# Halved additions for a pass's last operand, a unit issued in two parts, and two turns put with other work

## The chip, the core and the metric

The kernel runs on one core of a Trainium2 chip. A core has a matrix engine (PE, with its weight loads shown as PEld), a vector engine (DVE), a scalar engine (ACT), a general one (POOL) and a queue that issues the transfers (SP). Each has its own queue of instructions, runs it in order, and waits for the others through semaphores. The metric is the device time of one execution in microseconds (us), as a median of several runs. Beside the timed runs there is one profiled execution, whose span and time are given below.

## The reference

The kernel computes two layers of an encoder trunk for one sequence of 512 tokens of width 1024, all in float32. Cut to what matters here:

```python
for i in range(DEPTH):                        # 2 layers
    h = rms_norm(x, attn_norm[i])
    proj = h @ w_in[i]                        # one projection, its columns shared out
    mix = diff_attention(...) if i % 2 == 0 else gla_attention(...)
    cross = memory_cross_attention(mem_q, mem, mem_norm[i], w_mem_kv[i], mem_qk_norm[i])
    x = x + concatenate([mix, cross]) @ w_out[i]
    h = rms_norm(x, ffn_norm[i])
    x = x + conv_ffn(h, w_up[i], conv_w[i], conv_b[i], w_down[i])
# conv_ffn: u = h @ w_up, a causal convolution of width 3, silu(g) * a, and then @ w_down
# memory_cross_attention: 256 memory tokens, normalised, then @ w_kv gives keys and values
```

The inner width of the feed-forward part is 2816, that is 22 blocks of 128 columns for each of `a` and `g`.

## The kernel before

**Products.** Every large product is made of three: an operand is split into a rounded part (`hi`, written by ACT) and the remainder (`lo`, a subtraction on DVE), and PE adds hi x hi, hi x lo and lo x hi in PSUM. For weights, `split_weights` does this (L255 on ACT, L258 on DVE); for the combined weights below it is `combined` (sums on POOL at L287 to L290, roundings at L291 and L294, remainders at L292 and L295). A weight tile has 1024 columns, six of each kind are kept (`WB`), and a new block is made when PE has used an old one up (`make_block`, called from `freed` and `refill`).

**The feed-forward part** (`ffn`) runs in three passes over the inner width, of 4, 4 and 3 double blocks (`HALVES`). A pass first makes its inner operands: for each double block q, `up` multiplies (L387 to L389, in `product`), `conv` applies the convolution (L1166 to L1170), ACT the silu (L1329), and DVE multiplies (L1330). Then `down` multiplies by `w_down` and adds to x.

**The seven products.** Except in layer 0's last pass, and for one of the last pass's four output pairs in layer 1, a 2 x 2 block of `down` is computed with seven products instead of eight. That takes sums of the operand blocks: `combine` forms four sums of 256 columns into a tile `tsum` of 1024 (L1199 to L1202), and `parts_of` splits that tile (L1191 on ACT, L1192 on DVE). The sums are made on POOL, but on DVE for the last double block of a pass (`V if q == base + nq - 1 else ADD`). Of the seven steps, number 0 uses the second inner block's left half, 1 and 2 the first block's halves, and 3, 4, 5 and 6 use the sums q[3], q[0], q[1] and q[2]. Those four are called the mixed steps here.

**The order in `down`.** The output has four pairs of blocks (c = 0 to 3), and each has a unit of seven steps (21 products of 256 columns, L1247, routine `seven`) for every double block m. Pair c holds four PSUM banks; c and c + 2 use the same ones. The units are issued as follows: all of pair 0 but the last, pair 1's first, pair 0's last, the rest of pair 1, then pairs 2 and 3. When a pair's last unit has been issued, `decode` adds its four banks to x (L1256 on ACT, L1257 to L1264 on DVE), after which the banks are free. `release` follows each unit and lets `refill` make further weight blocks.

**Layer 0's attention.** PE's work is written out by hand in `SCRIPT`. A number pops that many microseconds' worth of projection units off a queue of work (`Filler`; a unit is six products of 512 columns, L365 to L367). Letters stand for attention work: `L` and `M` the logits of a group (L771), `T` its turn (four transposes on PE, L222, then a copy on ACT, L800), `V` its values (L812, which read that copy), `N` a normalisation (ACT squares at L422, sums and scales on DVE), `P` the transposes of the next head, `a` the memory operands. The queue holds, in this order, the values' projection, the second queries and keys, the memory's keys and values (`kv`, two blocks of four units), and further ones. At the end of that projection's first block a hook calls `token_rsqrt`, which computes the memory's scales (two transposes on PE, a sum at L468 on DVE, then ACT and DVE); the outputs of both blocks are scaled by them.

**What sets the order.** Only PE's queue is in the order of the program (`manual_schedule(engines={PE})`). For ACT, DVE, POOL and SP a planner orders the instructions ahead of time, by its own cost estimates and with program order as the priority. So an instruction that it takes to be waiting can be overtaken by later ones, and an order once planned is kept on the chip.

Of the kernel before, what the change touches and what calls it, by code (L numbers as in the profile page):

```python
# [21 lines left out]
S = 512  # L22
# [17 lines left out]
    17.75 P0 3.9  # L40
    L0 M1 a3 3.4 P1 5.05 a0 0.97
    1.94 a1 T0
    L2 M3 a2 3.57
    T1 4.86 N2 V0 T2 N3 V1 12.33
    L4 P2 4.55 P3 1.62 V2 T3 2.27 T4
    L5 M6 s0 V3 b1 2.6 V4 1.3 T5 1.3
    L7 M8 3.5 T6 F0 3.64 b0
# [135 lines left out]
def trunk(ctx, tc, head_d, x_t, mem_t, wpack, cols_a_d, cols_d, conv_d, gate_d, rel_bias, diff_lambda, consts, onehot, out):  # L183
    nc = tc.nc
    mm = nc.tensor.matmul
    V, A, G = nc.vector, nc.scalar, nc.gpsimd
# [23 lines left out]
    def blk(b, w=128):  # L210
        return slice(w * b, w * b + w)
# [140 lines left out]
    def gemm(sh, sl, nb, key, w, evac, hook=None, late=False, spare=False):  # L352
        got, open_ = [], {}

        piece = [q[0] for q in plan].index(key)

        def unit(b, k0, k1):
            if not got:
                got.extend(weights(key, True))
            if k0 == 0:  # L360
                open_[b] = bank("tp" if spare and b == 0 else "lg" if late and b > 1 else "mm")[:, :w]
            p = open_[b]
            for k in range(k0, k1):
                hi, lo = got[k]
                mm(p, sh[k][:, blk(b)], hi, start=k == 0, stop=False)  # L365
                mm(p, sh[k][:, blk(b)], lo, start=False, stop=False)  # L366
                mm(p, sl[k][:, blk(b)], hi, start=False, stop=k == KT - 1)  # L367
                if b == nb - 1:
                    freed(piece, k)
            if k1 == KT:  # L370
                if hook is not None and b == 0:
                    hook()
                evac(b, open_.pop(b))
        units = [(b, k) for b in range(nb) for k in range(0, KT, 2)]
        if late:
            units.sort(key=lambda u: u[0] == nb - 1 or u[1] == KT - 2)
        for b, k in units:
            F.add(6 * w / 2370.0, lambda b=b, k=k: unit(b, k, k + 2))
# [24 lines left out]
    r_mem = perm.tile([128, 2], F32, name="r_mem")  # L403
# [60 lines left out]
    def token_rsqrt(tag, sq, nb, y, on_dve=False):  # L464
        p, ss = bank(tag), small("ss")[:, :nb]
        for b in range(nb):
            transpose(p[:, blk(b)], sq[:, blk(b)])
        V.reduce_sum(ss, p[:, :128 * nb].rearrange("p (b n) -> p b n", b=nb), axis=AX.X)  # L468
        return rsqrt(ss, nb, 1.0 / D, on_dve, y=y)
# [9 lines left out]
    E = mybir.EngineType  # L479
# [106 lines left out]
    def mem_kv(l):  # L586
        hs, ls = [None] * KT, [None] * KT
        km = [None]

        def operands(ks=range(KT)):  # L590
            if l == 0 and km[0] is None:
                mem_squares()
            if km[0] is None:
                km[0] = xtile().rearrange("p (b n) -> p b n", b=2)
            for k in ks:
                if k % 2 == 0:
                    mh, ml = split_tiles()
                c = blk(k % 2, 256)
                hs[k], ls[k] = mh[:, c], ml[:, c]
                split(hs[k], ls[k], memT[k // 2][:, c], c_mem(l, k))  # L600

        def ev(b, p):
            A.activation(km[0][:, b], p[:, :256], AF.Copy, scale=r_mem[:, b:b + 1])
            A.activation(vm[l][:, b], p[:, 256:], AF.Copy, scale=r_mem[:, b:b + 1])

        def keys(tag="lg"):
            F.need(f"kv{l}")
            p = bank(tag)
            for hp in range(2):
                for b in range(2):  # L610
                    transpose(p[:, 256 * hp + 128 * b:256 * hp + 128 * b + 128], km[0][:, b, blk(hp)])
            A.activation(kmT[l].rearrange("p a b -> p (a b)"), p, AF.Copy, scale=c_mk(l))
        gemm(hs, ls, 2, ("kv", l), 512, ev,
             (lambda: token_rsqrt("lg", mem_acc[0], 2, r_mem)) if l == 0 else None)
        F.add(0.0, lambda: group_norm(None, km[0], 2, 4, 64))
        F.mark(f"kv{l}")
        return operands, keys
# [79 lines left out]
    def diff_layer(pool, mix, acc):  # L697
# [154 lines left out]
        for key in ORDER:  # L852
# [19 lines left out]
            "N": lambda i: norms(i // 2, i % 2), "a": lambda i: ops[0]((2 * i, 2 * i + 1)),  # L872
            "b": lambda i: ops[1]((2 * i, 2 * i + 1)), "k": lambda i: keys[i]("sm"),
            "q": lambda i: ma.queries() if i else (F.need("v2"), ma.norm()),
            "l": lambda i: ma.logits(i), "t": ma.turn, "v": lambda i: ma.values(i, "sm"),
            "s": lambda i: scales.pop(i)(), "X": lambda i: load_x(x_t),
            "O": lambda i: last.append(out_proj(0, mix, 1, acc, 5)), "!": lambda i: F.flush()}
        do(SCRIPT, doing)
# [270 lines left out]
    def ffn(pool, l, acc):  # L1149
# [40 lines left out]
        def parts_of(t, hi, lo):  # L1190
            A.copy(hi, t)  # L1191
            V.tensor_sub(lo, t, hi.bitcast(F32))  # L1192
# [3 lines left out]
        def combine(b2, b1, bh, bl, fh, fl, E):  # L1196
            t = pool.tile([128, 2 * S], F32, name="tsum", bufs=1)
            q = [blk(i, 256) for i in range(4)]
            E.tensor_sub(t[:, q[0]], b1[:, right], b1[:, left])  # L1199
            E.tensor_sub(t[:, q[1]], b2[:, right], t[:, q[0]])  # L1200
            E.tensor_sub(t[:, q[2]], b2[:, right], b1[:, right])
            E.tensor_sub(t[:, q[3]], b2[:, left], t[:, q[1]])  # L1202
            h, lo = (pool.tile([128, 2 * S], F32R, name="mid2", bufs=9) for _ in range(2))
            parts_of(t, h, lo)
            two = lambda hi, lw, c: (hi[:, c], lw[:, c])
            return [(fh, fl), two(bh, bl, left), two(bh, bl, right), two(h, lo, q[3]),
                    two(h, lo, q[0]), two(h, lo, q[1]), two(h, lo, q[2])]

        place = [(2, left), (0, left), (0, right), (1, left), (1, right), (2, right), (3, left)]
        steps, close = (1, 2, 0, 5, 6, 3, 4), {2: 0, 5: 2, 6: 3, 4: 1}  # L1210

        def down(base, nq, mids, pairs, tags, last, acc2):
            first = used[0]
# [21 lines left out]
            def release(c, m):  # L1235
                nonlocal live
                piece = first + c
                if m == nq - 1 or m % 2:
                    live -= 1 if whole[c] else 2
                    refill()  # L1240

            def seven(c, m):
                for i in steps:
                    b, h = place[i]
                    (hi, lo), (bh, bl) = made[first + c][m][i], mids[m][i]
                    for t, (w, v) in enumerate(((hi, bh), (hi, bl), (lo, bh))):
                        mm(banks[c][b][:, h], w, v, start=b not in seen[c], stop=m == nq - 1 and t == 2 and i in close)  # L1247
                        seen[c].add(b)
                release(c, m)
                if m == nq - 1:  # L1250
                    made[first + c] = None
                    decode(c)
# [35 lines left out]
                        made[first + c] = None  # L1288
                return
            refill()  # L1290
            seq = [(0, m) for m in range(nq - 1)] + [(1, 0), (0, nq - 1)] + [(1, m) for m in range(1, nq)]
            seq += [(2, m) for m in range(nq)] + ([] if whole[3] else [(3, m) for m in range(nq)])
            for c, m in seq:
                if c not in banks:
                    start(c)
                seven(c, m)
            if whole[3]:
                start(3)
                while done[0] < first_of[first + 4]:
# [140 lines left out]
```

## Time and profile before

| what | value |
|---|---|
| median of 3 runs | 1156.9 us (1156.76 to 1157.95) |
| profiled execution, its own time | 1156.94 us |
| its span in the profile | 1153.9 us |
| PE busy | 1145.4 us (99%) |
| DVE busy | 871.9 us (76%) |
| ACT busy | 590.7 us (51%) |
| POOL busy | 196.5 us (17%) |

A row of the timeline gives the start from the span's beginning, the duration (both in us), the engine, the line of the kernel, the operation, what it writes and reads with sizes, and how many like it are merged; in brackets stands how long the engine was idle before it and for whom it waited. Matrix products overlap each other: the next may start before the bar of the last one ends, so idle time on PE is best read from the distance of two starts. A list of waits gives the sum in us, the number and the longest. The five closings of passes that use the seven products lie, by L1247's rows, at 328.9 to 370.8, 458.0 to 498.8, 883.0 to 924.3, 1011.5 to 1052.4 and 1117.8 to 1142.2 us.

### The profile page before, as it was taken

Reading aid. Unit: us, or ns where it says so; the run is one execution under the profiler, and the core shown is the slowest. Engines: PE = TensorE matmul, PEld = TensorE weight load, DVE = VectorE, ACT = ScalarE, POOL = GpSimd, SP = SyncE. Lnnn points to the kernel's source line nnn. Section 1 sums busy time; section 2 is a strip of 40 time slices with the busy share of each in tenths; the row PEclk is TensorE's granted clock in tenths of the full one; section 3 lists DMA queues with packets and bytes.
Section 4 is the critical chain, followed back from the end, with each engine's and each line's share of the span. In section 5 each row is a group of like instructions: output and inputs, shape, how many; then the busy total and the mean of one; then the engine's idle time right before and its main releaser. Section 6 shows DMA issues by size and latency. Waiting matters only on the chain.

```text
span 1153.9 us, 16645 instructions
## 1 busy us (share of the span) xinstructions
PE 1145.4 (99%) x6311; PEld 986.5 (85%) x6311; DVE 871.9 (76%) x1450; ACT 590.7 (51%) x1027; POOL 196.5 (17%) x230
## 2 busy tenths in 40 slices
PE   9999999999999999999999999999999999999998
PEld 7888888888889888988888888988888988899887
DVE  8576778688689677977677637777887977797777
ACT  6676687555354344434457634435644444443442
POOL 0000000001543125500000000000144403370340
PEclk9999999999999999999999999999999999999999
DMA  8522242233214322243252220333241442233312
GB/s 294 169 80 86 79 142 74 59 106 115 87 59 143 110 76 80 101 135 103 69 179 71 97 98 9 108 122 113 77 124 38 130 143 73 68 93 132 93 45 101
DMA packets 39661, 117.81 MB, mean 102 GB/s; under 512 B 4767, under 2 KB 7256, under 8 KB 39582
## 3 DMA queue, kind: packets, MB, share of 16 engines
q1 hardware_dynamic: 39150, 116.37, 31.4%
q8 instruction: 49, 0.80, 0.3%
q10 hardware_dynamic: 432, 0.39, 0.1%
q14 instruction: 30, 0.25, 0.1%
HBM read 112.54 MB, written 4.21 MB: 101 GB/s over the span
## 4 chain that ended last, share of the span: by engine, by line
PE 77%; DVE 12%; POOL 5%; ACT 3%; DMA 2%; issue 2%; ACTq 0%; DVEq 0%; POOLq 0%
PE ps_mm L365 6%; PE ps_mm L367 6%; PE ps_mm L366 6%; PE ps_mm L387 5%; PE ps_mm L388 5%; PE ps_mm L389 5%; PE ps_lg L1247 4%; PE ps_sm L387 3%; PE ps_sm L388 3%; PE ps_sm L389 3%; PE ps_tp L1247 3%; PE ps_tp L222 3%; PE ps_mm L1247 2%; PE ps_lg L387 2%; PE ps_lg L389 2%; PE ps_lg L388 2%
## 5 line engine op out<-in xcount | busy, mean ns | idle before, releaser
L258 DVE TENSOR_TENSOR wlo<-raw,whi 128x1024 fp32r<-128x1024 f32 (+4 forms) x174 | 194.4, 1128 | 75.6 <-ACT whi L255 74.7
L255 ACT CAST whi<-raw 128x1024 fp32r<-128x1024 f32 (+4 forms) x174 | 168.1, 976 | 112.7 <-PE ps_sm L388 29.7
L365 PE MATMUL ps_mm<-whi,xsh 128*128 128x512 f32 (+2 forms) x328 | 126.4, 385 | 0.0
L367 PE MATMUL ps_mm<-whi,xsl 128*128 128x512 f32 (+2 forms) x328 | 123.0, 375 | 0.0
L366 PE MATMUL ps_mm<-wlo,xsh 128*128 128x512 f32 (+2 forms) x328 | 122.8, 374 | 0.0
L387 PE MATMUL ps_mm<-xsh,whi 128*128 128x512 f32 x278 | 109.3, 393 | 0.0
L388 PE MATMUL ps_mm<-xsl,whi 128*128 128x512 f32 x278 | 108.3, 390 | 0.0
L389 PE MATMUL ps_mm<-xsh,wlo 128*128 128x512 f32 x278 | 108.3, 389 | 0.0
L387 PE MATMUL ps_sm<-xsh,whi 128*128 128x512 f32 x218 | 84.8, 389 | 0.0
L388 PE MATMUL ps_sm<-xsl,whi 128*128 128x512 f32 x218 | 84.8, 389 | 0.0
L389 PE MATMUL ps_sm<-xsh,wlo 128*128 128x512 f32 x218 | 84.8, 389 | 0.0
L365 PEld LDWEIGHTS ps_mm<-whi,xsh 128*128 128x128 f32 x328 | 61.7, 188 | 11.4 <-issue 1.0
L367 PEld LDWEIGHTS ps_mm<-whi,xsl 128*128 128x128 f32 x328 | 61.7, 188 | 11.3
L366 PEld LDWEIGHTS ps_mm<-wlo,xsh 128*128 128x128 f32 x328 | 61.8, 188 | 10.1
L387 PE MATMUL ps_lg<-xsh,whi 128*128 128x512 f32 x160 | 62.2, 389 | 0.0
L388 PE MATMUL ps_lg<-xsl,whi 128*128 128x512 f32 x160 | 62.2, 389 | 0.0
L389 PE MATMUL ps_lg<-xsh,wlo 128*128 128x512 f32 x160 | 62.2, 389 | 0.0
L387 PE MATMUL ps_tp<-xsh,whi 128*128 128x512 f32 x160 | 62.2, 389 | 0.0
L388 PE MATMUL ps_tp<-xsl,whi 128*128 128x512 f32 x160 | 62.2, 389 | 0.0
L389 PE MATMUL ps_tp<-xsh,wlo 128*128 128x512 f32 x160 | 62.2, 389 | 0.0
L389 PEld LDWEIGHTS ps_mm<-xsh,wlo 128*128 128x128 f32 x278 | 52.2, 188 | 11.0
L388 PEld LDWEIGHTS ps_mm<-xsl,whi 128*128 128x128 f32 x278 | 52.2, 188 | 10.7 <-DVE xsl L346 0.4
(382 smaller groups left out, 2833.3 us busy)
## 6 DMA issues: line engine op xcount, KB each, us to landing
raw<-in_wpack_dram SPq DMA_DIRECT2D x178, 512.0 KB, 3.5
xt<-in_x_t_dram SPq DMA_DIRECT2D x15, 256.0 KB, 5.3
raw<-in_wpack_dram SPq DMA_DIRECT2D x15, 256.0 KB, 3.2
raw<-in_wpack_dram SPq DMA_DIRECT2D x8, 384.0 KB, 3.1
xres<-xt SPq DMA_DIRECT2D x8, 256.0 KB, 3.3
xt<-xres SPq DMA_DIRECT2D x8, 256.0 KB, 5.3
out_dram<-xt SPq DMA_DIRECT2D x7, 256.0 KB, 2.0
bt<-bias_d SPq DMA_DIRECT2D x6, 256.0 KB, 4.2
```

The lines of the kernel that those rows point to most:

```text
L222: nc.tensor.transpose(dst, src, ident[:n, :n])
L255: ins = A.copy(hi[:, c], raw[:, c])
L258: V.tensor_sub(lo[:, c], raw[:, c], hi[:, c].bitcast(F32))
L365: mm(p, sh[k][:, blk(b)], hi, start=k == 0, stop=False)
L366: mm(p, sh[k][:, blk(b)], lo, start=False, stop=False)
L367: mm(p, sl[k][:, blk(b)], hi, start=False, stop=k == KT - 1)
L387: mm(p, hi[:, blk(n)], bh, start=i == first, stop=False)
L388: mm(p, hi[:, blk(n)], bl, start=False, stop=False)
L389: mm(p, lo[:, blk(n)], bh, start=False, stop=i == last)
L1247: mm(banks[c][b][:, h], w, v, start=b not in seen[c], stop=m == nq - 1 and t == 2 and i in close)
```

## The change

There are three edits.

1. **Halves.** In `combine`, when the sums are made on DVE (the last double block of a pass), `parts_of` is called twice, on columns 0 to 511 (q[0], q[1]) and 512 to 1023 (q[2], q[3]), instead of once on all 1024. The steps' order becomes 1, 2, 0, 5, 4, 6, 3 (it was 1, 2, 0, 5, 6, 3, 4), so that the two mixed steps of the first half come before those of the second. This order holds in all units. A bank is now closed by step 3 where it was by step 4.
2. **A unit in two parts.** `seven` can issue some of its steps. Pair 0's last unit issues steps 1, 2 and 0; pair 1's second unit then issues its own 1, 2 and 0; then come the four mixed steps of pair 0's last unit and the four of pair 1's second. `release` and `decode` follow the second part.
3. **Turns.** In `SCRIPT` the turn T1 goes from its own place in the middle of a stretch of projection to behind V0, T2 and V1 go behind a further 2.6 us of projection, and a new letter `w` calls `token_rsqrt` for the memory's scales right behind V1; the hook in the memory's projection is dropped. The numbers between add up to 20.76 as they did.

```diff
@@ -40,8 +40,8 @@
     17.75 P0 3.9
     L0 M1 a3 3.4 P1 5.05 a0 0.97
     1.94 a1 T0
-    L2 M3 a2 3.57
-    T1 4.86 N2 V0 T2 N3 V1 12.33
+    L2 M3 a2 8.43
+    N2 V0 T1 N3 2.6 T2 V1 w 9.73
     L4 P2 4.55 P3 1.62 V2 T3 2.27 T4
     L5 M6 s0 V3 b1 2.6 V4 1.3 T5 1.3
     L7 M8 3.5 T6 F0 3.64 b0
@@ -610,8 +610,7 @@
                 for b in range(2):
                     transpose(p[:, 256 * hp + 128 * b:256 * hp + 128 * b + 128], km[0][:, b, blk(hp)])
             A.activation(kmT[l].rearrange("p a b -> p (a b)"), p, AF.Copy, scale=c_mk(l))
-        gemm(hs, ls, 2, ("kv", l), 512, ev,
-             (lambda: token_rsqrt("lg", mem_acc[0], 2, r_mem)) if l == 0 else None)
+        gemm(hs, ls, 2, ("kv", l), 512, ev)
         F.add(0.0, lambda: group_norm(None, km[0], 2, 4, 64))
         F.mark(f"kv{l}")
         return operands, keys
@@ -872,7 +871,7 @@
             "N": lambda i: norms(i // 2, i % 2), "a": lambda i: ops[0]((2 * i, 2 * i + 1)),
             "b": lambda i: ops[1]((2 * i, 2 * i + 1)), "k": lambda i: keys[i]("sm"),
             "q": lambda i: ma.queries() if i else (F.need("v2"), ma.norm()),
-            "l": lambda i: ma.logits(i), "t": ma.turn, "v": lambda i: ma.values(i, "sm"),
+            "w": lambda i: token_rsqrt("lg", mem_acc[0], 2, r_mem), "l": lambda i: ma.logits(i), "t": ma.turn, "v": lambda i: ma.values(i, "sm"),
             "s": lambda i: scales.pop(i)(), "X": lambda i: load_x(x_t),
             "O": lambda i: last.append(out_proj(0, mix, 1, acc, 5)), "!": lambda i: F.flush()}
         do(SCRIPT, doing)
@@ -1201,13 +1200,14 @@
             E.tensor_sub(t[:, q[2]], b2[:, right], b1[:, right])
             E.tensor_sub(t[:, q[3]], b2[:, left], t[:, q[1]])
             h, lo = (pool.tile([128, 2 * S], F32R, name="mid2", bufs=9) for _ in range(2))
-            parts_of(t, h, lo)
+            for c in ((blk(0, S), blk(1, S)) if E is V else (blk(0, 2 * S),)):
+                parts_of(t[:, c], h[:, c], lo[:, c])
             two = lambda hi, lw, c: (hi[:, c], lw[:, c])
             return [(fh, fl), two(bh, bl, left), two(bh, bl, right), two(h, lo, q[3]),
                     two(h, lo, q[0]), two(h, lo, q[1]), two(h, lo, q[2])]
 
         place = [(2, left), (0, left), (0, right), (1, left), (1, right), (2, right), (3, left)]
-        steps, close = (1, 2, 0, 5, 6, 3, 4), {2: 0, 5: 2, 6: 3, 4: 1}
+        steps, close = (1, 2, 0, 5, 4, 6, 3), {2: 0, 5: 2, 6: 3, 3: 1}
 
         def down(base, nq, mids, pairs, tags, last, acc2):
             first = used[0]
@@ -1239,13 +1239,15 @@
                     live -= 1 if whole[c] else 2
                     refill()
 
-            def seven(c, m):
-                for i in steps:
+            def seven(c, m, some=steps):
+                for i in some:
                     b, h = place[i]
                     (hi, lo), (bh, bl) = made[first + c][m][i], mids[m][i]
                     for t, (w, v) in enumerate(((hi, bh), (hi, bl), (lo, bh))):
                         mm(banks[c][b][:, h], w, v, start=b not in seen[c], stop=m == nq - 1 and t == 2 and i in close)
                         seen[c].add(b)
+                if some[-1] != steps[-1]:
+                    return
                 release(c, m)
                 if m == nq - 1:
                     made[first + c] = None
@@ -1288,12 +1290,14 @@
                         made[first + c] = None
                 return
             refill()
-            seq = [(0, m) for m in range(nq - 1)] + [(1, 0), (0, nq - 1)] + [(1, m) for m in range(1, nq)]
-            seq += [(2, m) for m in range(nq)] + ([] if whole[3] else [(3, m) for m in range(nq)])
-            for c, m in seq:
+            own, mixed = steps[:3], steps[3:]
+            seq = [(0, m, steps) for m in range(nq - 1)] + [(1, 0, steps), (0, nq - 1, own), (1, 1, own), (0, nq - 1, mixed)]
+            seq += [(1, 1, mixed)] + [(1, m, steps) for m in range(2, nq)]
+            seq += [(c, m, steps) for c in ((2,) if whole[3] else (2, 3)) for m in range(nq)]
+            for c, m, some in seq:
                 if c not in banks:
                     start(c)
-                seven(c, m)
+                seven(c, m, some)
             if whole[3]:
                 start(3)
                 while done[0] < first_of[first + 4]:
```

## The prediction

> **What bounds the kernel now.** I read the page first (part 1), then the waits of the matrix engine (PE), then the timeline around each of them.
>
> ```profile
> span 1153.9 us, 16645 instructions
> ...
> PE 1145.4 (99%) x6311; PEld 986.5 (85%) x6311; DVE 871.9 (76%) x1450; ACT 590.7 (51%) x1027; POOL 196.5 (17%) x230
> ```
>
> PE is nearly always occupied and its queue runs in the written order, so time is won only where PE stands still or gets less work. The list of PE's own waits, over the whole span, is this short (sum, times, longest):
>
> ```profile
> PE ps_sm L1247 <- DVE mid L1192: 3.1, 4, 1.4
> PE ps_tp L1247 <- DVE mid L1192: 0.9, 1, 0.9
> ...
> PE ps_tp L1247 <- ACT mid L1191: 0.5, 1, 0.5
> ```
>
> The line left out is the program's start (L492). The rest are in L1247, the units of seven products that close a pass, and wait for the conversion of the last operand (L1191 the rounded copy on ACT, L1192 the remainder on DVE). They understate the loss, because a product's bar is longer than its turn. The timeline of the first such place shows it:
>
> ```profile
> 337.49 0.41 DVE L1200 TENSOR_TENSOR tsum<-cvo,tsum 128x256 f32<-128x256 f32 x1
> ...
> 338.16 0.41 DVE L1202 TENSOR_TENSOR tsum<-cvo,tsum 128x256 f32<-128x256 f32 x1
> ...
> 338.50 0.94 DVE L292 TENSOR_TENSOR wlo<-raw,whi 128x768 fp32r<-128x768 f32 x1
> ...
> 338.60 1.05 ACT L1191 CAST mid<-tsum 128x1024 fp32r<-128x1024 f32 x1 [0.87 <-DVE tsum L1202]
> ...
> 339.68 0.40 PE L1247 MATMUL ps_sm<-mid,whi 128*128 128x256 f32 x2
> ...
> 339.92 0.28 PE L1247 MATMUL ps_sm<-mid,wlo 128*128 128x256 f32 x1
> 340.04 0.28 PE L1247 MATMUL ps_sm<-mid,whi 128*128 128x256 f32 x1
> 340.50 1.21 DVE L1192 TENSOR_TENSOR mid<-tsum,mid 128x1024 fp32r<-128x1024 f32 x1
> ...
> 341.76 0.38 PE L1247 MATMUL ps_sm<-mid,whi 128*128 128x256 f32 x1 [1.45 <-DVE mid L1192]
> ```
>
> From 339.68 three products take 0.36 us: one turn is 0.12 us. The product after 340.04 was due at 340.16 and started at 341.76: 1.60 us lost, which is the idle time shown plus 0.16 (a bar of 0.28 less a turn of 0.12). It is the second product of step 5, the first that reads the remainder; the one at 340.04 needs only the rounded copy. The remainder was late because DVE, while ACT rounded, had begun two subtractions for weights (L292, and L295 behind it). The other four places:
>
> ```profile
> 469.76 0.38 PE L1247 MATMUL ps_sm<-mid,whi 128*128 128x256 f32 x1 [0.37 <-DVE mid L1192]
> ...
> 895.29 0.39 PE L1247 MATMUL ps_sm<-mid,whi 128*128 128x256 f32 x1 [0.90 <-DVE mid L1192]
> ...
> 1023.34 0.39 PE L1247 MATMUL ps_sm<-mid,whi 128*128 128x256 f32 x1 [0.42 <-DVE mid L1192]
> ...
> 1127.04 1.23 DVE L1192 TENSOR_TENSOR mid<-tsum,mid 128x1024 fp32r<-128x1024 f32 x1
> ...
> 1127.06 0.38 PE L1247 MATMUL ps_tp<-mid,whi 128*128 128x256 f32 x1 [0.49 <-ACT mid L1191]
> 1128.32 0.38 PE L1247 MATMUL ps_tp<-mid,whi 128*128 128x256 f32 x1 [0.88 <-DVE mid L1192]
> ```
>
> With 0.16 more each they lose 0.53, 1.06 and 0.58; the last pass waits twice, 0.49 + 0.16 = 0.65 and 0.88 + 0.38 - 0.12 = 1.14, together 1.79. With the first place that is 5.56 us of standstill. Layer 0's last pass closes with undivided blocks (the routine `eight`) and has none.
>
> **The change, part by part.**
>
> *The last unit in two parts.* In each of the five passes, output pair 0's last unit now issues steps 1, 2, 0 (9 products, none reading the mixed operand), then pair 1's second unit issues its own 9, then the mixed steps 5, 4, 6, 3 of both. No product is added or dropped. The first mixed step comes 9 x 0.12 = 1.08 us later in PE's queue, and PE works meanwhile: pair 1's banks are open from its unit 0, and the weights of its units 0 and 1 come in one block. With the old finishing times the standstills would shrink to 1.60 - 1.08 = 0.52, 0, 0, 0, and 1.79 - 1.08 = 0.71: 1.23 left, 4.33 won by this alone.
>
> *The halves.* One ACT and one DVE instruction of 1024 columns become two each of 512, only for the last operand of a pass (the others stay on POOL's route). The price of a half, from neighbours of the same width:
>
> ```profile
> 1007.77 0.62 ACT L1191 CAST mid<-cvo 128x512 fp32r<-128x512 f32 x1 [0.78 <-DVE cvo L1330]
> ...
> 1008.42 0.69 DVE L1192 TENSOR_TENSOR mid<-cvo,mid 128x512 fp32r<-128x512 f32 x1
> ```
>
> ACT pays 2 x 0.62 - 1.05 = 0.19 us more and DVE 2 x 0.69 - 1.21 = 0.17 us more a pass, 1.8 us over five. I cost that at nothing: ACT is busy 51% and DVE 76%, and PE has other products meanwhile; without that cover it would be those 1.8 at most. The gain: the first half needs only L1199 and L1200, done at 337.90 in the first pass, so its copy can run there until 338.55 instead of waiting for L1202 (338.57). Its remainder is then ready when DVE leaves L1202, ahead of L292, and done by about 339.3. Steps 5 and 4 read just this half, from 340.16 + 1.08 = 341.24 on; steps 6 and 3 read the other, 6 x 0.12 = 0.72 us later.
> Even if both halves stay behind L292 and L295 and start at 340.50, they end at 341.19 and 341.88, before 341.24 and 341.96. In the last pass the same worst case starts at 1127.04, and the first half ends at 1127.73 against 1127.61 (1127.06 less 0.65, plus one turn, plus 1.08): 0.12 late, with a hand-over of 0.05 (341.71 to 341.76) 0.17. So 0 to 0.17 us are left. That a reader of one half isn't held by the other is seen at the program's start, where PE uses one half of a weight tile while the other is written:
>
> ```profile
> 4.07 1.64 PE L566 MATMUL ps_mm<-whi,xsh 128*128 128x256 f32 x4
> ...
> 4.57 0.29 DVE L528 CAST whi<-raw 128x256 fp32r<-128x256 f32 x1 [0.65 <-DMA raw<-in_wpack_dram]
> ```
>
> I take 0.06 left, nearer to the early case since DVE and ACT both have room there: 5.50 won by both edits.
>
> *What is late next.* PE reaches pair 2 up to 1.8 us sooner. There it needs the next weights (POOL's sums L287 to L290, ACT, then L295) and the banks that pair 0's last additions free (L1261 the last).
>
> ```profile
> 344.97 1.43 DVE L295 TENSOR_TENSOR wlo<-wsum,whi 128x1024 fp32r<-128x1024 f32 x1
> 346.33 0.68 DVE L1261 TENSOR_TENSOR xt<-xt,ps_mm 128x512 f32<-128x512 f32 x1
> ...
> 350.74 0.40 PE L1247 MATMUL ps_mm<-mid,whi 128*128 128x256 f32 x2
> ...
> 1131.52 1.22 DVE L295 TENSOR_TENSOR wlo<-wsum,whi 128x1024 fp32r<-128x1024 f32 x1
> ...
> 1134.77 0.40 PE L1247 MATMUL ps_lg<-mid,whi 128*128 128x256 f32 x2
> ```
>
> In the first pass pair 2 would start at 350.74 - 1.60 = 349.14; the weights are done at 346.40 and the banks at 347.01. In the last it starts at 1132.98 and reads the summed weights' remainder 5 turns later, 1133.58; that is done at 1132.74, and if half a subtraction (0.69) goes ahead on DVE, at 1133.43. Margins of 2.1 and 0.15: no new wait, costed at nothing. SP's loads and POOL's sums follow buffers that these same products free: pair 0's last block 1.08 later in PE's queue, pair 1's first block 12 products behind it instead of 21, both before pair 2. The new order of the steps (bank 1 now closes with step 3) changes no count.
>
> *The turns in layer 0.* T1 (four transposes) moves from a place of its own to behind V0; T2 and V1 move behind two more projection units; and the two transposes for the memory's scales (`w`) leave the end of the first memory block and join them. Three places between projections become two.
>
> ```profile
> 74.19 0.60 PE L222 MATMUL ps_tp<-C,xt 128*128 128x128 f32 x4
> 74.55 0.49 PE L365 MATMUL ps_mm<-whi,xsh 128*128 128x512 f32 x1
> 74.87 0.39 PE L366 MATMUL ps_mm<-wlo,xsh 128*128 128x512 f32 x1
> 75.11 0.39 PE L367 MATMUL ps_mm<-whi,xsl 128*128 128x512 f32 x1
> ...
> 78.77 1.05 PE L812 MATMUL ps_sm<-vv,xt 128*128 128x128 f32 x8
> 79.66 0.60 PE L222 MATMUL ps_tp<-C,xt 128*128 128x128 f32 x4
> 80.10 1.06 PE L812 MATMUL ps_sm<-vv,xt 128*128 128x128 f32 x8
> ...
> 82.21 0.57 ACT L800 COPY xt<-ps_tp 128x512 f32<-128x512 f32 x1
> ...
> 82.79 1.14 ACT L422 ACTIVATE xt<-ks 128x512 f32<-128x512 f32 x2
> ```
>
> The return to projections costs 0.32 - 0.24 = 0.08 us (74.55, 74.87, 75.11). One return fewer saves 0 to 0.08; I take 0.05. Behind T1 stands a new wait: V1 reads T1's copy. T1 alone took 0.36 + 0.08 = 0.44; without it PE comes to V0 at 78.33, ends V0 (0.89) and T1 (0.44) at 79.66, does 12 products (2.88 at 0.24) and T2 (0.44), and reaches V1 at 82.98. T1 takes the place in the order that T2 had, whose copy ended at 82.78. So V1 finds it ready by 0.2 us, if ACT keeps this order: 0 to 0.1 lost, 0 taken. T2's own copy is wanted only by V2, later. `w` goes earlier than its readers need.
>
> **Sum.** The profiled execution took 1156.94 us, 0.04 over the median of the runs shown and 3.0 over its span; those 3.0 are left as they are. 1156.94 - 5.50 - 0.05 = 1151.39: **1151.4 us**, 0.48% less.
>
> **The rivals.**
>
> *A, the halves help less.* They keep the whole's place on DVE, which leaves 0.17 (above), or a reader of one half is held by both. Then step 5 waits for the second half, 0.17 later than the old whole: 341.93 against 341.24 is 0.69; the passes at 469 and 1023 lose none (their 0.53 and 0.58 plus 0.17 are under 1.08); 1.06 + 0.17 - 1.08 = 0.15; and 1.79 + 0.17 - 1.08 = 0.88. Together 1.72, 1153.1 us. For it speaks that DVE did take two weight subtractions first; against it the rows of the program's start.
> The Trainium skill, "VectorE: DVE Perf Modes", section "The TRN2 errata — SBUF-src ops pay a fixed extra latency per instruction", says that each vector instruction pays a fixed time, so cutting one up is dearer; by its formula (N + 151)/0.96 two halves come 158 ns above one whole. The 0.17 of the rows agrees; it speaks against this edit, and A is the most that it can do here.
>
> *B, V1 waits.* ACT puts T1's copy behind N3's two squares (1.14): it ends at 83.92, PE stands 1.0 us, 1152.4.
>
> *C, the gain is taken back at pair 2.* PE would have to wait there 3.2 us or more of the 5.5. With 2.1 us of margin in the first pass that takes sums or additions reordered by over 2 us in most passes. Then about 1155.5, no difference that counts.
>
> *D, slower.* The wait of B, with the copy behind weight roundings that themselves wait for buffers and loads:
>
> ```profile
> 88.70 1.03 ACT L255 CAST whi<-raw 128x1024 fp32r<-128x1024 f32 x1
> ...
> 90.36 1.99 ACT L255 CAST whi<-raw 128x1024 fp32r<-128x1024 f32 x2
> ```
>
> Behind all three the copy would end at 92.9, PE would lose 10 us from 82.98, and the time be 1161.4. It decides from a copy later than 82.98 + 5.5 + 2.3 = 90.8. Against it: T2's copy stood ahead of all three.
>
> **How the numbers follow.** This kernel's measurement can tell about 0.2% (2.3 us) from no change. Forecast 0.62, A 0.14, B 0.12: faster, 0.88. C 0.06: same. D 0.06: slower. The forecast's own range is 1150.9 to 1152.0, its bounds and as much again for the planner, whose order on ACT and DVE can't be read before. With A and B, alone or together (1151.4 + 1.7 + 1.0 = 1154.1), 1150.8 to 1154.0 holds some 0.87, which I keep for that reason.
>
> **What would show it.** Right: no PE wait for L1192 or L1191; pair 0's own steps followed without a gap by pair 1's; halves of about 0.62 and 0.69 with the first ahead of L292; V1 right after T2. Wrong: a wait of L1247 for `wlo`, `whi` or a bank at pair 2, a wait of L812 for L800 near 83, or more than 0.3 us of PE waits left at L1192.

## The result and the profile after

The changed kernel took 1149.63 us (median of 6 runs, 1149.08 to 1151.63) against 1156.92 for the kernel before (6 runs, 1155.65 to 1157.95). The ratio is 0.994, with a 95% interval of 0.9927 to 0.9953. The forecast was 1151.4 us with a range of 1150.8 to 1154.0: the direction was right, but the measured time lies 1.2 us below the lower end of the range.

The page of the changed kernel begins so; below it stands the beginning of the chain that ended last:

```profile
span 1148.5 us, 16655 instructions
...
PE 1142.7 (99%) x6311; PEld 985.1 (86%) x6311; DVE 871.2 (76%) x1455; ACT 592.0 (52%) x1032; POOL 193.2 (17%) x230
...
PE 99%; DMA 0%; DVE 0%; ACT 0%; issue 0%
```

PE has the same 6311 products. DVE and ACT have five instructions more each, one for each of the five passes. The whole chain is now PE: what released the last instruction goes back through PE's own queue nearly to the start. In the kernel before the same line of the page had 23% of other things in it:

```profile
PE 77%; DVE 12%; POOL 5%; ACT 3%; DMA 2%; issue 2%; ACTq 0%; DVEq 0%; POOLq 0%
```

PE's share of busy time was 99% in both kernels, so it tells nothing of the 6 us that were lost there; the list of PE's waits does. In the changed kernel it is:

```profile
PE ps_tp L492 <- PEq L1399: 0.8, 1, 0.8
PE ps_mm L566 <- DVE whi L528: 0.4, 1, 0.4
PE ps_mm L566 <- ACT xsh L345: 0.2, 1, 0.2
```

All three belong to the program's first microseconds. The four rows of the seven products (L1247, as before) are gone, and none for pair 2 or for the values (L811, which was L812) has come in their place. Lines are a little shifted: the copy of the last operand is now L1190, its remainder L1191, the sums L1198 to L1201. The first pass in the timeline:

```profile
337.23 1.29 ACT L1190 CAST mid<-tsum 128x512 fp32r<-128x512 f32 x2 [0.19 <-DVE tsum L1199]
...
337.79 0.95 DVE L292 TENSOR_TENSOR wlo<-raw,whi 128x768 fp32r<-128x768 f32 x1
...
338.66 1.28 DVE L1191 TENSOR_TENSOR mid<-tsum,mid 128x512 fp32r<-128x512 f32 x2
...
339.22 0.28 PE L1247 MATMUL ps_sm<-mid,wlo 128*128 128x256 f32 x1
339.34 0.40 PE L1247 MATMUL ps_lg<-mid,whi 128*128 128x256 f32 x2
...
339.86 1.21 DVE L295 TENSOR_TENSOR wlo<-wsum,whi 128x1024 fp32r<-128x1024 f32 x1
...
340.30 0.28 PE L1247 MATMUL ps_tp<-mid,wlo 128*128 128x256 f32 x1
340.42 0.40 PE L1247 MATMUL ps_sm<-mid,whi 128*128 128x256 f32 x2
340.66 0.28 PE L1247 MATMUL ps_sm<-mid,wlo 128*128 128x256 f32 x1
```

Pair 0's own products end with the one at 339.22, pair 1's nine begin 0.12 us later at 339.34, and the mixed steps follow at 340.42 = 339.34 + 9 x 0.12. There is no gap: the next row, at 340.66, is the third product of the first mixed step, on time. Both halves of the remainder run back to back from 338.66 and are done at 339.94: behind the weight subtraction L292, but ahead of L295. PE reads the first half at 340.54 and the second some 0.72 later, so there is over 1 us to spare (about 1.2 for the first half and 1.3 for the second). The last pass:

```profile
1120.99 0.68 DVE L1191 TENSOR_TENSOR mid<-tsum,mid 128x512 fp32r<-128x512 f32 x1
...
1121.59 0.54 DVE L292 TENSOR_TENSOR wlo<-raw,whi 128x384 fp32r<-128x384 f32 x1
...
1122.06 0.68 DVE L1191 TENSOR_TENSOR mid<-tsum,mid 128x512 fp32r<-128x512 f32 x1
...
1122.51 0.28 PE L1247 MATMUL ps_sm<-mid,wlo 128*128 128x256 f32 x1
1122.63 0.40 PE L1247 MATMUL ps_tp<-mid,whi 128*128 128x256 f32 x2
```

Here the first half goes ahead of L292 and the second behind it; the mixed steps start at 1122.63 without a wait.

**Where the time went.** The same product, found in both traces by its number in PE's order, gives how far PE is ahead at each point. Over the five closings PE gains 1.70, 0.62, 1.15, 0.67 and 1.88 us, together 6.02. The rest of this pair of executions is small: 0.54 up to the last product of the program's start (L566, at 27.93 before and 27.39 after, of which more below), 0.05 at the moved turns with another 0.05 just behind them (up to 97.5 us), and under 0.1 elsewhere. PE's last product starts 6.74 us earlier:

```profile
1150.47 0.28 PE L389 MATMUL ps_sm<-mid,wlo 128*128 128x256 f32 x1
```

in the kernel before, and in the changed one

```profile
1143.73 0.28 PE L389 MATMUL ps_sm<-mid,wlo 128*128 128x256 f32 x1
```

From there to the end of the execution it took 1156.94 - 1150.47 = 6.47 us before and 1150.36 - 1143.73 = 6.63 us after.

### The profile page after: what moved, and what is told of

It reads as the page before. It is cut to its first block, busy times and chain, and to the rows that moved or that the text cites. A ratio compares the mean times of both kernels' runs of the same rounds, so it can differ in the third digit from the quotient of the medians.

```text
span 1148.5 us, 16655 instructions
## 1 busy us (share of the span) xinstructions
PE 1142.7 (99%) x6311; PEld 985.1 (86%) x6311; DVE 871.2 (76%) x1455; ACT 592.0 (52%) x1032; POOL 193.2 (17%) x230
## 4 chain that ended last, share of the span: by engine, by line
PE 99%; DMA 0%; DVE 0%; ACT 0%; issue 0%
PE ps_mm L365 6%; PE ps_mm L367 6%; PE ps_mm L366 6%; PE ps_mm L387 6%; PE ps_mm L388 6%; PE ps_mm L389 6%; PE ps_lg L1247 5%; PE ps_sm L388 5%; PE ps_sm L389 5%; PE ps_sm L387 5%; PE ps_mm L1247 4%; PE ps_tp L388 4%; PE ps_lg L388 4%; PE ps_tp L387 4%; PE ps_lg L387 4%; PE ps_tp L389 4%
## 5 line engine op out<-in xcount | busy, mean ns | idle before, releaser
L387 PEld LDWEIGHTS ps_mm<-xsh,whi 128*128 128x128 f32 x278 | 52.2, 188 | 10.8 <-issue 0.3
```

The source lines that it names most:

```text
L387: mm(p, hi[:, blk(n)], bh, start=i == first, stop=False)
```

## The experiments

The kernels ran in three groups, each on one chip together with the kernel before: the first four with 21 runs of it (median 1156.13 us), the next four with 15 (1155.96), the last one with 9 (1156.81).

**The kernel before against itself.** A line of comment is added; it shows what a difference of nothing looks like.

```diff
+# the same kernel
```

> The kernel before with one comment line more, so nothing changes. The changed kernel's profile has three terms that the sum did not have: 0.6 us less before the first projection ends (27.93 to 27.39), 1.25 us more behind the last product, and 1.2 us less outside the span (3.04 to 1.86). Theory 1 (these vary from one execution or chip to the next, whatever the kernel): several of this control's executions differ from one another by about as much, and its time minus span lies near 2.0 as the changed kernel's does on the same chip. Theory 2 (the change makes them): this control keeps 3.0 outside the span and 27.9 at the start. In both the ratio to the kernel before is 1.000 within 0.001, and the five standstills are 1.70, 0.62, 1.15, 0.67 and 1.88 us again.

Measured: 1155.85 us (11 runs), ratio 0.9999 (0.9991 to 1.0008). In its trace all five standstills are as before and PE's last product comes at 1150.36, 0.11 earlier. Behind that product it has 1157.07 - 1150.36 = 6.71 us. So the time outside the span varies without any change (1.84 here against 2.99), as theory 1 said; the start of the program, 27.81, is nearly that of the kernel before. What follows: PE's stream repeats to about 0.1 us, while the medians of one and the same program lie between 1155.85 and 1156.81 from group to group; the forecast started from 1156.94.

**The last unit in two parts, alone** (edit 2, added to the kernel before):

```diff
...
-            seq = [(0, m) for m in range(nq - 1)] + [(1, 0), (0, nq - 1)] + [(1, m) for m in range(1, nq)]
...
+            own, mixed = steps[:3], steps[3:]
+            seq = [(0, m, steps) for m in range(nq - 1)] + [(1, 0, steps), (0, nq - 1, own), (1, 1, own), (0, nq - 1, mixed)]
+            seq += [(1, 1, mixed)] + [(1, m, steps) for m in range(2, nq)]
...
```

> Only the last unit in two parts; whole 1024-column conversion, old order of the steps, old script. By the prediction's working 0.52 us are left in the first pass and 0.71 in the last, and nothing in the other three: 4.33 us won. Theory 1 adds about 0.1 us for each wait, that is 0.1 for each of the three that vanish: about 4.6 us less than the kernel before (0.40%). Rival (each edit needs the other, for instance because the planner moves the conversion back by as much as PE comes later): under 2 us.

Measured: 1151.16 us (5 runs), ratio 0.9956 (0.9942 to 0.9969). The closings gain 1.07, 0.62, 1.07, 0.67 and 1.08, together 4.51. Two waits are left, in the first and in the last pass (the list of PE's waits, and the places in the timeline):

```profile
PE ps_tp L1247 <- DVE mid L1192: 0.5, 1, 0.5
PE ps_sm L1247 <- DVE mid L1192: 0.4, 1, 0.4
```

```profile
340.68 0.28 PE L1247 MATMUL ps_sm<-mid,whi 128*128 128x256 f32 x1
...
341.33 0.39 PE L1247 MATMUL ps_sm<-mid,whi 128*128 128x256 f32 x1 [0.36 <-DVE mid L1192]
341.55 0.28 PE L1247 MATMUL ps_sm<-mid,wlo 128*128 128x256 f32 x1
...
1123.61 0.28 PE L1247 MATMUL ps_tp<-mid,whi 128*128 128x256 f32 x1
...
1124.43 0.38 PE L1247 MATMUL ps_tp<-mid,whi 128*128 128x256 f32 x1 [0.54 <-DVE mid L1192]
```

341.33 - 340.68 - 0.12 = 0.53 and 1124.43 - 1123.61 - 0.12 = 0.70 us: the 0.52 and 0.71 that the prediction had left for this edit alone.

**The halves alone** (edit 1 with its order of steps, added to the kernel before):

```diff
-            parts_of(t, h, lo)
+            for c in ((blk(0, S), blk(1, S)) if E is V else (blk(0, 2 * S),)):
+                parts_of(t[:, c], h[:, c], lo[:, c])
...
-        steps, close = (1, 2, 0, 5, 6, 3, 4), {2: 0, 5: 2, 6: 3, 4: 1}
+        steps, close = (1, 2, 0, 5, 4, 6, 3), {2: 0, 5: 2, 6: 3, 3: 1}
```

> Only the halves and the new order of the steps; units whole, old script. In the profile of the changed kernel the first half's remainder is done 0.7 us after DVE leaves L292, ahead of L295. If the planner keeps that order here, step 5 finds it in four of five passes, and the last pass waits about 0.4 us for its second half: about 5.5 us less than before, nearly all of the gain, so that the two edits overlap. Rival (the halves help little alone, as both stay behind L292 and L295): the first half ends 0.5 us sooner than the whole did, and 2.3 us are won.

Measured: 1150.42 us (5 runs), ratio 0.9948 (0.9935 to 0.996). The closings gain 1.67, 0.62, 1.15, 0.67 and 1.38, together 5.49. Only the last pass still stands, twice and for so short that the list of waits has no row for it. It shows in merged pairs of products that are longer than the usual 0.40:

```profile
1122.16 0.56 PE L1248 MATMUL ps_tp<-mid,whi 128*128 128x256 f32 x2
...
1123.03 0.76 PE L1248 MATMUL ps_tp<-mid,whi 128*128 128x256 f32 x2
```

They are 0.16 and 0.36 us too long, 0.52 together (in each about 0.10 is the slow restart that is explained below), where the whole kernel gains 1.88 - 1.38 = 0.50 more. So the halves alone, with their order of the steps, do nine tenths of the work (5.49 of 6.02), and parts and halves mostly remove the same waits: added up, the two alone would have made 10.0.

**The turns alone** (edit 3, added to the kernel before):

```diff
-    L2 M3 a2 3.57
-    T1 4.86 N2 V0 T2 N3 V1 12.33
+    L2 M3 a2 8.43
+    N2 V0 T1 N3 2.6 T2 V1 w 9.73
...
```

> Only the script: T1 behind V0, T2 and V1 later, w behind V1. Theory: one return from transposes to projections fewer, 0.05 us, no wait of V1 for T1's copy, ratio 1.000 within 0.001. Theory 2 (the turns are worth more than the rows say, and carry the 1.2 us that the sum lacked): 1.2 us less, ratio 0.999.

Measured: 1155.96 us (11 runs), ratio 0.9997 (0.9988 to 1.0006). The waits stay as they were in the first four passes (below) and in the last, and none is added:

```profile
PE ps_sm L1246 <- DVE mid L1191: 3.0, 4, 1.4
...
```

PE's last product starts 0.37 us earlier than before. Of that, 0.07 lies in the program's start and 0.05 at the moved groups; another 0.05 follows by 97.5 us in all five kernels that have this edit and in none of the five others that were compared with before, so it belongs to the edit, though why isn't known. The other 0.2 us are not found again in the changed kernel, and nothing here says what they are.

**The changed kernel beside the kernel before** (the changed kernel with one line of comment), for a comparison on the same chip:

> The changed kernel with one comment line more, beside the kernel before on one chip. Theory 1 (PE gains the five standstills with their restarts, 6.02 us, and 0.05 from the turns; the rest of the first comparison was in how executions differ outside PE's work): about 6.1 us less at the median, ratio 0.9947. Theory 2 (the change wins 7.3 us): ratio 0.9937. The interval may hold both; then the spans decide, with 1153.7 before less 6.1 or less 7.3.

Measured: 1149.71 us (1149.58 to 1149.79, 5 runs), ratio 0.9945 (0.9933 to 0.9958). The closings gain the same 6.02. The difference to the 15 runs of before is 6.25 us, and that of the median spans 1154.0 - 1147.7 = 6.3: theory 1.

**The changed kernel without the turns** (edits 1 and 2):

```diff
-    L2 M3 a2 8.43
-    N2 V0 T1 N3 2.6 T2 V1 w 9.73
+    L2 M3 a2 3.57
+    T1 4.86 N2 V0 T2 N3 V1 12.33
...
```

> Halves and two parts, old script. Theory: as the changed kernel within 0.1 us, that is 6.0 us less than before; PE has no wait at L1247. If the turns carried a part of the gain, this one is slower than the changed kernel by that part.

Measured: 1149.96 us (5 runs), ratio 0.9948 (0.9935 to 0.9962), with the same 6.02 at the closings and no wait of L1247. The turns are worth 0.25 us or less by the medians, 0.07 by where PE's last product starts (1144.33 against 1144.26).

**The halves with the old order of the steps.** Here the first two mixed steps read both halves one after the other:

```diff
-        steps, close = (1, 2, 0, 5, 4, 6, 3), {2: 0, 5: 2, 6: 3, 3: 1}
+        steps, close = (1, 2, 0, 5, 6, 3, 4), {2: 0, 5: 2, 6: 3, 4: 1}
```

This line stands against the kernel with the halves alone; parts and turns are left out.

> Halves with the old order of the steps (5, 6, 3, 4), units whole, old script: the step after the first half's first step now needs the second half. With the finishing times seen in the run with the halves alone, the second half comes 0.2 us late in the first pass and about 0.9 in the last: about 0.6 us worse than the halves with the new order, so 4.9 less than before. Rival (the order of the steps is worth nothing, because PE takes the halves as one): the same as with the new order.

Measured: 1150.63 us (5 runs), ratio 0.9953 (0.9941 to 0.9966). The closings gain 1.43, 0.62, 1.15, 0.67 and 1.02, together 4.89: the order of the steps is worth 0.60 us where there are no parts, in the first and the last pass. The last pass shows the reason:

```profile
1122.94 0.68 DVE L1192 TENSOR_TENSOR mid<-tsum,mid 128x512 fp32r<-128x512 f32 x1
1122.94 0.28 PE L1248 MATMUL ps_tp<-mid,whi 128*128 128x256 f32 x1
...
1123.67 0.39 PE L1248 MATMUL ps_tp<-mid,whi 128*128 128x256 f32 x1 [0.45 <-DVE mid L1192]
1123.89 0.28 PE L1248 MATMUL ps_tp<-mid,wlo 128*128 128x256 f32 x1
```

The product at 1123.67 is of step 6, the second mixed step in this order. It reads the second half, whose remainder ends at 1123.62; with the new order PE would still have had the step that reads the first half. So a product that reads one half does run before the other half is written (step 5 did), as the rows of the program's start had suggested.

**Every half converted twice.** The changed kernel with the copy and the remainder made a second time, with the same result:

```diff
-                parts_of(t[:, c], h[:, c], lo[:, c])
+                for _ in range(2 if E is V else 1):
+                    parts_of(t[:, c], h[:, c], lo[:, c])
```

> The changed kernel with both conversions of the last operand done twice, each copy and each subtraction writing the same numbers again: 1.2 us more on ACT and 1.3 us more on DVE in each of five passes, ahead of PE's mixed steps. It measures the cover under which the extra 0.19 and 0.17 us a pass were costed at nothing. Theory: PE waits some 0.2 to 0.3 us in the first and the last pass and hardly in the others, under 1 us in all against the changed kernel. Rival (what is added to these conversions lies on the path): 5 x 1.3 = 6.4 us, the whole gain lost.

Measured: 1154.25 us (1153.42 to 1155.09, 11 runs), ratio 0.9982 (0.9974 to 0.9991). The closings gain only 0.41, 0.35, 0.26, 0.41 and 0.64, together 2.07: 3.95 less than the changed kernel, which neither expectation had. The first pass:

```profile
339.69 1.28 DVE L1191 TENSOR_TENSOR mid<-tsum,mid 128x512 fp32r<-128x512 f32 x2
...
340.40 1.22 ACT L1190 CAST mid<-tsum 128x512 fp32r<-128x512 f32 x2 [0.84 <-DVE mid L1191]
...
340.89 1.21 DVE L295 TENSOR_TENSOR wlo<-wsum,whi 128x1024 fp32r<-128x1024 f32 x1
...
342.03 1.28 DVE L1191 TENSOR_TENSOR mid<-tsum,mid 128x512 fp32r<-128x512 f32 x2
...
342.76 0.39 PE L1248 MATMUL ps_sm<-mid,whi 128*128 128x256 f32 x1 [1.03 <-DVE mid L1191]
```

The second copy overwrites what the first remainder reads, so it has to wait for it; DVE takes L295 meanwhile, and the second remainders come 2.3 us after the first. It is a serial chain over two engines and not just twice the instructions. So the run does not price the 0.36 us a pass that the halves add. It shows that their cover ends: the parts put nine products, 1.08 us, ahead of the mixed steps, and with the remainders this late PE loses 1.29, 0.27, 0.89, 0.26 and 1.24 us against the changed kernel. The median span is 1151.6, 2.4 below before's, while the time is only 1.7 below: in nine of the eleven executions 2.5 us or more lie outside the span (more on this below).

**T1 directly ahead of V1.** The changed kernel with T1's 12 products of cover taken away:

```diff
-    N2 V0 T1 N3 2.6 T2 V1 w 9.73
+    N2 V0 N3 2.6 T2 T1 V1 w 9.73
```

> The changed kernel with T1 put last ahead of V1 (T2, T1, V1 instead of T1, 12 products, T2, V1), so that V1 has to wait for a copy of 0.57 us on ACT that has only just become possible. Theory (the 2.9 us of products between T1 and V1 are the cover that keeps rival B away): the matrix engine stands still in front of V1 by 0.6 us at least (the copy and a hand-over) and by up to 1.7 if two squares of 0.57 each go ahead on ACT, a wait of L812 for L800 appears in the list of waits, and the time rises by the same 0.6 to 1.7 against the changed kernel (span some 4.6 to 5.7 below before, where the changed kernel's is 6.3 below). Rival (the place of T1 does not matter, since PE can hide the copy behind the loads of V1's weights or the products before it): no such wait, 0.1 us or less.

Measured: 1151.32 us (1151.17 to 1151.39, 5 runs), ratio 0.9956 (0.9942 to 0.9969). The median span is 1149.3, 1.6 more than the changed kernel's 1147.7 and 4.5 less than that of before on the same chip (1153.8), just outside the 4.6 to 5.7 that was expected. The list of waits has the row that rival B would have had, and the timeline the copies it waits for:

```profile
PE ps_sm L811 <- ACT xt L799: 1.2, 1, 1.2
```

```profile
82.25 0.50 ACT L243 ACTIVATE rs_y<-ss,eps 128x16 f32<-128x16 f32 x2
82.67 0.34 ACT L244 ACTIVATE rs_y<-rs_y 128x16 f32<-128x16 f32 x2
82.91 1.05 ACT L799 COPY xt<-ps_tp 128x512 f32<-128x512 f32 x2
...
84.02 1.16 PE L811 MATMUL ps_sm<-vv,xt 128*128 128x128 f32 x8 [1.19 <-ACT xt L799]
```

The two copies come one behind the other, and PE waits for the second. From there on PE's stream is 1.39 us later than in the repeated changed kernel. So V1 does stand still when T1's copy is late, as rival B says, and B's 1.0 us was of the right order. What goes ahead of the copy here is T2's copy and four short functions of a normalisation, not the two squares that B named. In the changed kernel the 12 products between give the copy its time.

## Why the prediction was right in kind and too small in size

Two terms of the sum failed. The standstills were taken 0.52 us too small, counting the 0.06 left for a late half; this is shown. The 3.0 us outside the span were carried over unchanged and came out about 1 us lower; why stays open. With the first put right the forecast would have been 1150.87, just inside the range. With the second put right alone it would have been 1150.4, below the range.

**The standstills.** The place, the number and the cause were right: all five are gone, and the parts alone left what the working said (0.53 and 0.70 against 0.52 and 0.71). The sizes were not. I took 1.60, 0.53, 1.06, 0.58 and 1.79 and the products gained 1.70, 0.62, 1.15, 0.67 and 1.88: each 0.09 to 0.10 more (in the last pass the 0.38 in my working already held the first of its two restarts). The missing term is the restart. In the kernel before the product behind the wait starts at 341.76 and the next one, the first row here, 0.23 us later, not 0.12:

```profile
341.99 0.28 PE L1247 MATMUL ps_sm<-mid,wlo 128*128 128x256 f32 x1
342.10 0.40 PE L1247 MATMUL ps_sm<-mid,whi 128*128 128x256 f32 x2
```

The bar of 0.38 instead of 0.28 stood in the fences of the prediction, and only its start was read. The rows of the weight loads show what differs. At the usual pace a product's weights begin to load with the product ahead of it (the load below at 339.80 is for the product at 339.92); those of the product at 341.76 begin to load only with it:

```profile
339.80 0.19 PEld L1247 LDWEIGHTS ps_sm<-mid,wlo 128*128 128x128 f32 x1
...
341.76 0.19 PEld L1247 LDWEIGHTS ps_sm<-mid,whi 128*128 128x128 f32 x1 [1.65 <-DVE mid L1192]
```

That the 0.10 us are this load, not made ahead, fits the rows, but no run tested it. The size of the restart is shown again by the experiments: 341.33 to 341.55 with the parts alone, 1123.67 to 1123.89 with the old steps, 0.22 each. "5.56 us of standstill" should have been 6.02, and "5.50 won by both edits" 6.02 as well, since the 0.06 that I left for a late half did not come either.

**The time outside the span: the step that failed most.** The sum says "those 3.0 are left as they are". For the profiled pair that is nearly so, if what lies behind PE's last product is taken as a whole (6.47 and 6.63). But it isn't the same in every execution of a kernel: in the 45 runs of before it goes from 1.80 to 3.59 outside the span. Of the eleven profiled executions six have 5.3 to 5.6 us between PE's last product and the end, and five have 6.3 to 6.7; the kernel before and its control are among the latter, the repeated changed kernel among the former (1149.71 - 1144.26 = 5.45, from this row of its timeline, where the line is shifted by one):

```profile
1144.26 0.28 PE L390 MATMUL ps_sm<-mid,wlo 128*128 128x256 f32 x1
```

The extra 1 us or so lies outside the span in some executions (before: 2.99 there) and inside it in others (control: 4.88 from the last product to the span's end, against 3.48, and 1.84 outside). All three runs shown of before took 1156.76 or more; of the 45 runs in the three groups 15 did (4 of 21, 6 of 15 and 5 of 9). Of the changed kernel's six runs four took 1149.72 or less, below the profiled 1150.36, and all six have 1.86 to 2.22 us outside the span. So the sum began at an execution 0.8, 1.0 and 0.1 us above the medians of the three groups, and forecast the changed kernel in the same condition. Whether the kernel itself has a share in this is open. In favour: the kernel with every half converted twice has 2.5 us or more outside in nine of eleven executions, the changed kernel in none of its eleven, and before in 7 of 45. No run was made to separate it.

**The sum again.** From the forecast 1151.39 to the repeated changed kernel's 1149.71 are 1.68 us: 0.52 of closings; 2.99 - 1.97 = 1.02 outside the span; and some 0.15 in PE's stream, of which 0.09 is in the program's start and 0.06 more than forecast at the turns. In the first profiled execution of the changed kernel another 0.4 is the start of the program, where the first projection's last product began at 27.39 instead of 27.93. The repeated kernel, the same but for a comment, has it at 27.84, so this isn't the change's. Beside 15 runs of before on one chip the change is worth 6.25 us, about 0.54%; the first comparison's 7.3 has about 1 us of the ends in it.

**The halves.** That they cost nothing is borne out: with them and the parts PE waits nowhere. Rival A (1153.1) has no support: the halves alone gain 5.49, more than the parts alone, and a product that reads one half isn't held by the other. The Trainium skill ("VectorE: DVE Perf Modes", "The TRN2 errata — SBUF-src ops pay a fixed extra latency per instruction") gives the formula (N + 151)/0.96, from which I estimated 158 ns for two halves above one whole (it is 157). I took 0.17 from the single bars, and the formula fits those: 0.69 at 512 columns by both. Back to back the instructions cost less: from 338.66 until DVE starts L295 at 339.86 the two take 1.20 us, and in the last pass a half holds DVE from 1120.99 to 1121.59, 0.60. The whole held it in the kernel before from 340.50 until the next row, 1.13:

```profile
341.63 0.67 DVE L1257 TENSOR_TENSOR xt<-xt,ps_mm 128x512 f32<-128x512 f32 x1
```

So two halves cost 0.07 us more a pass and not 0.17, because each bar's last 0.08 us lie beside the next one's start; the measurement decides. My detail "with the first ahead of L292" came true only in the last pass. In the first pass the planner put both behind L292; they were in time because L295 no longer stood ahead of them.

**Pair 2.** No new wait, as forecast, so rival C is out. In the first pass pair 2 begins 2.6 us behind the last subtraction that frees its first bank, in the last pass 0.3 us:

```profile
345.07 0.67 DVE L1263 TENSOR_TENSOR xt<-xt,ps_mm 128x512 f32<-128x512 f32 x1
...
348.34 0.40 PE L1247 MATMUL ps_mm<-mid,whi 128*128 128x256 f32 x2
...
1125.91 1.22 DVE L295 TENSOR_TENSOR wlo<-wsum,whi 128x1024 fp32r<-128x1024 f32 x1
1127.05 0.68 DVE L1263 TENSOR_TENSOR xt<-xt,ps_lg 128x512 f32<-128x512 f32 x1
...
1128.03 0.40 PE L1247 MATMUL ps_lg<-mid,whi 128*128 128x256 f32 x2
```

In the last pass the weights were the tight case of the prediction, with 0.15 us of margin by its dates. They are ready at 1127.13 and read from about 1128.63; it is the bank, ready at 1127.73, that comes nearest.

**The turns.** Worth 0.05 at the groups, as taken. V1 found T1's copy ready, but not by the predicted 0.2 us: the planner ran it earlier than T2's old place.

```profile
79.26 0.59 ACT L799 COPY xt<-ps_tp 128x512 f32<-128x512 f32 x1
...
82.27 1.06 PE L811 MATMUL ps_sm<-vv,xt 128*128 128x128 f32 x8
```

82.27 - 79.85 = 2.4 us of margin. B and D did not happen.

**The range.** Its lower end, 1150.8, allowed 0.6 us below the forecast for everything that could go better. The standstills alone take 0.5 of it, and the base on which all of it stood was uncertain by about 1 us, which no term of the range held.

## What to carry to other kernels

Where an engine is busy 99% of the time, read its waits and not its share, and take what a wait costs from start to start over the product behind it too: the restart belongs to it. Two edits that remove the same wait don't add up: cutting the late operand in halves, with the steps in their order, did 5.49 of the 6.02 us here and giving PE other products meanwhile 4.51, and the second only made the first safe in the last pass. When a few runs of a kernel are all the base there is, compare the time behind its last product with that of other executions before it is carried over unchanged, and put its spread into the range.

## What the runs showed of the hardware that was not expected

- After a wait on another engine the first product of 256 columns keeps PE for 0.22 to 0.23 us where 0.12 is usual. It is so in every listed wait of the seven products that has no second wait right behind it: 0.10 us for each, which the list of waits doesn't count. That list also leaves out short ones: the 0.16 and 0.36 us with the halves alone have no row.
- The time from PE's last product to the end fell into two groups about 1 us apart in the eleven profiled executions, 5.3 to 5.6 and 6.3 to 6.7, in kernels whose last instructions are the same. The difference is inside the span in some executions and outside in others. What makes it was not tried, and whether it is independent of the kernel is open.
- The start of the program differs by up to 0.5 us between executions of the same code but for a comment (27.39 and 27.84 for the same product). This too is left open.
